# Sample state updates of an SSD decoder step: x and B regrouped by sequence through DRAM, two updates on two 32-row strips of the array

## The chip, the cores and the metric

One core of one Trainium2 chip runs the whole program. The metric is the device time of one execution in microseconds, the median of three runs. The program uses TensorE (PE, with its weight loads shown as PEld), VectorE (DVE), ScalarE (ACT), GpSimd (POOL) and SyncE (SP), which issues most of the DMAs; ACT and POOL issue some too.

## What is computed

The reference is one inference step of a one-layer hybrid decoder, for a prompt of 256 tokens and for 64 sample tokens (8 sequences of 8 tokens, each with a recurrent state of its own). The part around the change is the SSD mixer: a recurrence with 32 heads of 64 channels in 4 groups of 8 heads, with a state of 128 per channel.

```python
# h_t = exp(dt_t a) h_{t-1} + dt_t x_t B_t^T,  y_t = h_t C_t
xdt = (x * dt[..., None])
decay_states = jnp.exp(da_cs[:, :, -1:] - da_cs)
states = jnp.einsum("bcsgn,bcsgr,bcsgrp->bcgrpn", bc, decay_states, xdt)
...
y_off = jnp.einsum("bctgn,bcgrpn,bctgr->bctgrp", cc, states_in, jnp.exp(da_cs))
```

For each of the 8 sample sequences and each of the 4 groups of heads, the new state (128 x 512) is the old one times a decay, plus the product of B (8 tokens x 128) and of x dt decay (8 tokens x 512). Around it stand the projections W_in, W_out, W_up and W_down, all in float32, which are most of the work.

## The kernel before

**The stream of weights.** Every projection is computed transposed: blocks of 128x128 of a weight are the stationary operand, and all 320 tokens (256 + 64) are the moving one. A weight arrives in slabs of 512 KB (`slab`, L110): SP loads one into `wraw`, ACT rounds it to float32r (`whi`, L118), and DVE takes the remainder (`wlo`, L120); each of the three has three buffers. `accumulate` (L127) then makes three matmuls of 128x320 (L129 to L131) for each block, 24 for a slab. I call these the stream; a slab and its load are numbered in the order of the loads (slab 134, load 140).

**The order.** A tile framework puts every engine's instructions into one fixed order when the program is built, by priorities and by its own estimate of times; semaphores enforce what depends on what. DMAs from SP and ACT share eight semaphores, so that a DMA also waits for the one that used its semaphore last. Background work stands in generators that `tick` (L141) advances by one step between slabs. The SSD work of group g is such a generator, `ssd(g)` (L733); it runs between the slabs of W_in and W_out.

**One group of heads** (L733 to L949). SP loads the states of the samples in pairs (`load_state`, L739): `sts[i]` holds sequences i and 4+i, in six buffers `st`; the fourth pair is loaded once the first is stored. x is turned to tokens by PE transposes into PSUM (L762 to L766). For the prompt (c = 0, 1) it is multiplied by dt into `xdt`. For the samples (c = 2, 3: sequences 0 to 3 and 4 to 7), `fourfold` (L359) lets ACT first copy the 32 tokens four times side by side, so that one transpose gives the tokens on four strips of 32 rows; `xq` is x dt decay (L772), and `xsp` holds its float32r part on two strips and the remainder on the other two. B has the same layout in `bsp`, made once for all groups (L714 to L725). Both are split so that a product of the two sums high and low parts over the rows.

Then comes, for each pair i of sequences, `begin(i)` and `end(i)` (L852 to L860):

- `with_c` (L812): four matmuls into `yo_ps`, the old state times C, each on one strip of 32 columns of the array.
- `picked` (L820): ACT multiplies `bsp` by a column of `bsel` that is 1 on the rows of sequence i of each half and 0 elsewhere, into `bm`. That is the mask: all 128 rows take part, and only those of one sequence count.
- `shrunk` (L825): POOL multiplies the two states by their decay.
- `grown` (L831): for each of the two halves h, one matmul of 128x512 `bm[:, h]` by `xsp[:, h]` into a PSUM bank (`up_ps`, L834), which DVE adds to the state (L836).
- `store_state` (L839): ACT issues the two stores.

Between these stand `s_ps` (L806, the state of the prompt's first chunk, which waits for `x0d`, made by POOL in L794), and later the prompt's own products (`y_ps`, L912, pairs of matmuls on the two halves of the array's columns) and `fin_ps` (L938). Small tiles of PSUM come from a pool of four banks (`misc`, L57).

The step sizes dt are made earlier (`steps`, L411) with five blocks of 128 tokens: two of the prompt, one of the samples, and two more that repeat the samples fourfold.

Of the kernel before, what the change touches and what calls it, by code (L numbers as in the profile page):

```python
# [17 lines left out]
P = 128  # L18
# [16 lines left out]
def hybrid_step(  # L35
# [38 lines left out]
    bsel = cp.tile([P, 4], F32, name="bsel")  # L74
# [4 lines left out]
    def masks():  # L79
        make_upper_triangular(nc, upper, 1.0, diag=True)  # L80
        make_lower_triangular(nc, later, 1.0, diag=False)
        make_block_diagonal(nc, bd2, TS)

        for r in range(4):
            rs = slice(32 * r, 32 * r + 32)
            pool.tensor_copy(bsel[rs], bd2[rs, rs].rearrange("p (b t) -> p b t", b=4)[:, :, 0])
        for r in range(2):
            rs = slice(64 * r, 64 * r + 64)
            dve.tensor_tensor(out=upper_s[rs], in0=upper[rs, rs], in1=bd2[rs, rs], op=ALU.mult)
        pool.memset(cmask, 1.0)  # L90
        cm4 = cmask.rearrange("p (h b) i -> p h b i", h=2)
        pool.affine_select(out=cm4, in_=cm4, pattern=[[0, 2], [-8, 4], [1, 32]],
                           compare_op=ALU.is_ge, fill=0.0, base=0, channel_multiplier=0)
        pool.affine_select(out=cm4, in_=cm4, pattern=[[0, 2], [8, 4], [-1, 32]],
                           compare_op=ALU.is_ge, fill=0.0, base=7, channel_multiplier=0)
# [259 lines left out]
    def by_token(ps, x, c):  # L355

        pe.transpose(ps, x[:, P * c:P * c + P], ident)

    def fourfold(out, x, i):  # L359

        act.copy(out.rearrange("p k (q t) -> p k q t", q=4), x[:, :, NP + 32 * i:NP + 32 * i + 32].unsqueeze(2).to_broadcast([P, 4, 4, 32]))
        return out

    with ExitStack() as mctx:
# [40 lines left out]
        dt = op.tile([P, 5, NH], F32, name="dt")  # L405
        nda = op.tile([P, 3, NH], F32, name="nda")
        dec = op.tile([P, 5, NH], F32, name="dec")
# [3 lines left out]
        def steps():  # L411
# [23 lines left out]
            for i in range(2):  # L435
                pool.tensor_copy(dtf[:NH, (3 + i) * P:(4 + i) * P].rearrange("p (q t) -> p q t", q=4),
                                 dtf[:NH, NP + 32 * i:NP + 32 * i + 32].unsqueeze(1).to_broadcast([32, 4, 32]))
            yield
            ps = misc("dt_ps")
            for c in range(5):  # L440
                pe.transpose(ps[:, NH * c:NH * c + NH], dtf[:NH, P * c:P * c + P], ident[:NH, :NH])
            H5 = 5 * NH
            dve.tensor_tensor(out=dt, in0=ps[:, :H5].rearrange("p (c h) -> p c h", c=5),
                              in1=bias_bc.unsqueeze(1).to_broadcast([P, 5, NH]), op=ALU.add)

            e = op.tile([P, 5, NH], F32, name="sp_e")
            q = dec
            z2 = tp.tile([P, NT], F32, tag="pv", name="sp_z2", bufs=4)[:, :5 * NH].rearrange("p (c h) -> p c h", c=5)
            act.activation(e, dt, AF.Abs)
# [11 lines left out]
            dve.scalar_tensor_tensor(out=dt, in0=dt, scalar=0.0, in1=q, op0=ALU.max, op1=ALU.add)  # L461
# [3 lines left out]
            dve.scalar_tensor_tensor(out=da, in0=dt, scalar=-1.0, in1=ea.unsqueeze(1).to_broadcast([P, 5, NH]),  # L465
# [37 lines left out]
            later_s = tp.tile([P, NT], F32, tag="pv", name="later_s", bufs=4)[:NS, :2 * P].rearrange("p (r q t) -> p r q t", r=2, q=4)  # L503
            for r in range(2):
                rs = slice(32 * r, 32 * r + 32)
                pool.tensor_tensor(out=later_s[:, r], in0=later[:NS, rs].unsqueeze(1).to_broadcast([NS, 4, 32]),
                                   in1=bd[:, rs].unsqueeze(1).to_broadcast([NS, 4, 32]), op=ALU.mult)
                pe.matmul(ps[:, (3 + r) * NH:(4 + r) * NH], later_s[:, r].rearrange("p q t -> p (q t)"), da[:NS, 2],
                          start=True, stop=True)
            act.activation(dec.rearrange("p c h -> p (c h)"), ps[:, :H5], AF.Exp)  # L510
            dve.tensor_tensor(out=dt[:, 3:5], in0=dt[:, 3:5], in1=dec[:, 3:5], op=ALU.mult)
# [194 lines left out]
        with tc.tile_pool(name="sd", bufs=1) as sd:  # L706
# [7 lines left out]
            for c in range(4):  # L714
                ps = misc("bt_ps")
                b4 = bT if c < 2 else fourfold(sd.tile([P, 4, P], F32, tag="xde", name="b4", bufs=2), bT, c - 2)
                for g in range(4):
                    by_token(ps[:, P * g:P * g + P], b4[:, g], c if c < 2 else 0)
                if c < 2:
                    act.copy(btok[:, c, :], ps)  # L720
                else:
                    b = bsp[:, c - 2]
                    act.copy(b, ps)
                    for rs in (slice(32, 64), slice(96, P)):
                        dve.tensor_tensor(out=b[rs], in0=ps[rs], in1=b[rs].bitcast(F32), op=ALU.subtract)  # L725
# [7 lines left out]
            def ssd(g):  # L733
# [5 lines left out]
                def load_state(i):  # L739

                    st = [sd.tile([P, 512], F32, tag="st", name="st", bufs=6) for _ in range(2)]
                    for h in range(2):
                        sp.dma_start(st[h], state_ssm[4 * h + i, g])
                    return st

# [10 lines left out]
                def times(out, ps, c, at=slice(0, P), h=slice(0, 8)):  # L756
                    n = h.stop - h.start
                    dve.tensor_tensor(out=by_head(out), in0=by_head(ps),
                                      in1=dt[at, c, h0 + h.start:h0 + h.stop].unsqueeze(2).to_broadcast([at.stop - at.start, n, 64]), op=ALU.mult)

                xsp = sd.tile([P, 2, 512], F32R, tag="xsp", name="xsp", bufs=1)
                for c in range(4):  # L762
                    ps = misc("xt_ps")
                    x4 = xs if c < 2 else fourfold(sd.tile([P, 4, P], F32, tag="xde", name="x4", bufs=2), xs, c - 2)
                    for j in range(4):
                        by_token(ps[:, P * j:P * j + P], x4[:, j], c if c < 2 else 0)  # L766
                    if c < 2:
                        times(xdt[:, c, :], ps, c)
                        continue
                    i = c - 2  # L770
                    xq = sd.tile([P, 512], F32, tag="xde", name="xq", bufs=2)
                    times(xq, ps, c + 1)  # L772
                    act.copy(xsp[:, i], xq)
                    dve.tensor_tensor(out=xsp[64:, i], in0=xq[64:], in1=xsp[64:, i].bitcast(F32), op=ALU.subtract)
                    for r in range(2):
                        at = slice(64 - 64 * r + 32 * i, 96 - 64 * r + 32 * i)
                        times(xdt[at, 2, 256 * r:256 * r + 256], ps[at, 256 * r:256 * r + 256], 2, at, slice(4 * r, 4 * r + 4))
# [25 lines left out]
                yield  # L803

# [7 lines left out]
                def with_c(i, st):  # L812

                    for r in range(2):
                        for h in range(2):
                            row = 64 * r + 32 * h
                            pe.matmul(ps_yo[row:row + 32, :256], cms[:, 4 * h + i, :], st[h][:, 256 * r:256 * r + 256],  # L817
                                      start=i == 0, stop=i == 3, tile_position=(0, row))

                def picked(i):  # L820
                    bm = sd.tile([P, 2, P], F32R, tag="bm", name="bm", bufs=2)
                    act.activation(bm, bsp[:, :, bs].bitcast(F32), AF.Copy, scale=bsel[:, i:i + 1])
                    return bm

                def shrunk(i, st):  # L825
                    with first():
                        for h in range(2):
                            pool.tensor_tensor(out=by_head(st[h]), in0=by_head(st[h]),
                                               in1=tote[:, h0:h0 + 8, 4 * h + i:4 * h + i + 1].to_broadcast([P, 8, 64]), op=ALU.mult)

                def grown(st, bm):  # L831
                    for h in range(2):
                        ps = misc("up_ps")
                        made = pe.matmul(ps, bm[:, h], xsp[:, h], start=True, stop=True)  # L834
                        with first():
                            dve.tensor_tensor(out=st[h], in0=st[h], in1=ps, op=ALU.add)  # L836
                    return made.ins

                def store_state(i, st, by=act):  # L839
                    for h in range(2):  # L840
                        by.dma_start(o_ssm_s[4 * h + i, g], st[h])
# [8 lines left out]
                bms = {}  # L850

                def begin(i):  # L852
                    with_c(i, sts[i])
                    bms[i] = picked(i)
                    shrunk(i, sts[i])

                def end(i, by=act):
                    made = grown(sts[i], bms.pop(i))
# [423 lines left out]
```

## Time and profile before

| | |
|---|---|
| median of three runs | 1796.03 us (1794.56 to 1798.4) |
| the profiled execution, its own time | 1796.18 us |
| its span | 1794.3 us |
| its granted TensorE clock, mean | 0.996 |
| HBM read and written | 275.71 MB and 14.82 MB |
| stage with the SSD work | about 430 to 845 us from the span's start |

The profile page counts busy time by engine, follows the chain of work that ended last, and groups instructions by line. A row of the timeline gives the start, the time from the first start to the last end, the engine, the line, the operation, the tiles (written <- read), the shape and the count; a wait stands in brackets with what ended it. A matmul's duration holds its way through the array as well, so what it takes from the PE is the time from its start to the next one's start.

### The profile page before, as it was taken

How to read it: one execution, taken by the hardware profiler on the slowest of the kernel's cores; microseconds unless marked ns; L12 is line 12 of the kernel's file. 1: busy time of each engine (PE TensorE's matmuls, PEld its weight loads, DVE VectorE, ACT ScalarE, POOL GpSimd, SP SyncE). 2: the span in 40 equal slices, each digit the busy share in tenths (PEclk: the TensorE clock that was granted, in tenths of full speed). 3: DMA queues.
4: the chain of work that ended last, by engine and by line, in shares of the span. 5: the costliest groups of instructions: out<-in, count | busy, mean ns of one | idle time of the engine just before them, and what ended most of it. 6: DMA issues, size and time to landing. Idle time of an engine off the chain costs nothing.

```text
span 1794.3 us, 31172 instructions
## 1 busy us (share of the span) xinstructions
PE 1774.6 (99%) x12200; PEld 1741.1 (97%) x12200; DVE 1185.2 (66%) x2048; ACT 797.8 (44%) x1107; POOL 293.2 (16%) x619
## 2 busy tenths in 40 slices
PE   9999999999999999999999999999999999999998
PEld 8999999999889898999999999999999999999997
DVE  5459664556987969677875474746566575656575
ACT  6444454334545446445555433343434343433335
POOL 3102200000431303104321010111101020101004
PEclk9999999999999999999999999999999999999999
DMA  8646544445665565554554545554554555454542
GB/s 279 193 142 192 161 145 153 154 153 180 198 196 187 166 222 163 172 170 145 167 156 154 151 147 155 154 151 148 155 153 146 152 155 152 149 150 154 153 150 101
DMA packets 222226, 292.56 MB, mean 163 GB/s; under 512 B 16672, under 2 KB 150656, under 8 KB 221888
## 3 DMA queue, kind: packets, MB, share of 16 engines
q1 hardware_dynamic: 209392, 268.12, 49.1%
q10 hardware_dynamic: 10304, 14.82, 2.3%
q0 software_dynamic: 2384, 7.64, 1.4%
q8 instruction: 96, 1.57, 0.4%
q14 instruction: 50, 0.41, 0.1%
HBM read 275.71 MB, written 14.82 MB: 162 GB/s over the span
## 4 chain that ended last, share of the span: by engine, by line
PE 91%; DVE 4%; DMA 3%; issue 1%; ACT 1%; POOL 0%; DVEq 0%; ACTq 0%; POOLq 0%
PE ps L129 20%; PE ps L131 19%; PE ps L130 19%; PE pd L129 9%; PE pd L131 9%; PE pd L130 9%; DMA wraw<-in_w_in 1%; DVE wlo L120 1%; DMA cs<-dacs_d 1%; PE y_ps L912 1%; PE yo_ps L817 0%; PE sg L670 0%; DVE cv L388 0%; PE up_ps L834 0%; DVE cs L897 0%
## 5 line engine op out<-in xcount | busy, mean ns | idle before, releaser
L120 DVE TENSOR_TENSOR wlo<-wraw,whi 128x1024 fp32r<-128x1024 f32 (+1 forms) x474 | 585.4, 1235 | 434.0 <-ACT whi L118 431.9
L118 ACT CAST whi<-wraw 128x1024 fp32r<-128x1024 f32 (+1 forms) x475 | 494.8, 1042 | 715.9 <-PE ps L130 431.5
L129 PE MATMUL ps<-h_hi,whi 128*128 128x320 f32 x2524 | 783.4, 311 | 4.8 <-ACT h_hi L346 2.1
L131 PE MATMUL ps<-h_hi,wlo 128*128 128x320 f32 x2524 | 781.3, 310 | 2.0 <-DVE wlo L120 1.9
L130 PE MATMUL ps<-h_lo,whi 128*128 128x320 f32 x2524 | 780.8, 309 | 0.0
L129 PEld LDWEIGHTS ps<-h_hi,whi 128*128 128x128 f32 x2524 | 475.1, 188 | 8.8 <-issue 2.9
L131 PEld LDWEIGHTS ps<-h_hi,wlo 128*128 128x128 f32 x2524 | 474.9, 188 | 3.8 <-DVE wlo L120 3.1
L130 PEld LDWEIGHTS ps<-h_lo,whi 128*128 128x128 f32 x2524 | 475.2, 188 | 0.7 <-DVE h_lo L546 0.2
L129 PE MATMUL pd<-fhi,whi 128*128 128x320 f32 x704 | 217.5, 309 | 0.0
L130 PE MATMUL pd<-flo,whi 128*128 128x320 f32 x704 | 217.5, 309 | 0.0
L131 PE MATMUL pd<-fhi,wlo 128*128 128x320 f32 x704 | 217.5, 309 | 0.0
L129 PE MATMUL pd<-ohi,whi 128*128 128x320 f32 x448 | 139.8, 312 | 0.0
L131 PE MATMUL pd<-ohi,wlo 128*128 128x320 f32 x448 | 138.8, 310 | 0.0
L130 PE MATMUL pd<-olo,whi 128*128 128x320 f32 x448 | 138.6, 309 | 0.0
L129 PEld LDWEIGHTS pd<-fhi,whi 128*128 128x128 f32 x704 | 132.4, 188 | 0.0
L130 PEld LDWEIGHTS pd<-flo,whi 128*128 128x128 f32 x704 | 132.4, 188 | 0.0
L131 PEld LDWEIGHTS pd<-fhi,wlo 128*128 128x128 f32 x704 | 132.4, 188 | 0.0
L1093 POOL COPY ptf<-pad 128x2 f32<-128x2 f32 x88 | 21.0, 239 | 622.3 <-DVE pad L1081 621.6
L217 DVE TENSOR_TENSOR acc_ffn<-acc_ffn,pd 128x320 f32<-128x320 f32 x160 | 77.5, 484 | 38.3 <-PE pd L131 36.9
L129 PEld LDWEIGHTS pd<-ohi,whi 128*128 128x128 f32 x448 | 84.1, 188 | 1.4 <-issue 0.6
L131 PEld LDWEIGHTS pd<-ohi,wlo 128*128 128x128 f32 x448 | 84.1, 188 | 0.5 <-issue 0.4
L130 PEld LDWEIGHTS pd<-olo,whi 128*128 128x128 f32 x448 | 84.1, 188 | 0.2
(301 smaller groups left out, 1590.3 us busy)
## 6 DMA issues: line engine op xcount, KB each, us to landing
wraw<-in_ffn_w_up SPq DMA_DIRECT2D x176, 512.0 KB, 3.7
wraw<-in_w_in SPq DMA_DIRECT2D x144, 512.0 KB, 3.7
wraw<-in_ffn_w_down SPq DMA_DIRECT2D x88, 512.0 KB, 3.5
wraw<-in_w_out SPq DMA_DIRECT2D x64, 512.0 KB, 3.5
st<-in_state_ssm SPq DMA_DIRECT2D x32, 256.0 KB, 4.1
out_ssm_state_sample<-st ACTq DMA_DIRECT2D x30, 256.0 KB, 3.5
cs<-dacs_d SPq DMA_DIRECT2D x16, 320.0 KB, 4.2
xr<-in_xT SPq DMA_DIRECT2D x4, 640.0 KB, 3.9
```

The source lines that it names most:

```text
L118: act.copy(hi[:, o], raw[:, o])
L120: dve.tensor_tensor(out=lo[:, :m], in0=raw[:, :m], in1=hi[:, :m].bitcast(F32), op=ALU.subtract)
L129: pe.matmul(ps, whi, xhi, start=first, stop=False)
L130: pe.matmul(ps, whi, xlo, start=False, stop=False)
L131: return pe.matmul(ps, wlo, xhi, start=False, stop=last).ins
L217: dve.tensor_tensor(out=acc[:, nb, :], in0=acc[:, nb, :], in1=ps[:, :NT], op=ALU.add)
L912: pe.matmul(ps[64 * i:64 * i + 64, cols], w(hl), x(hl, m, cpx), tile_position=(0, 64 * i), **flags)
L1093: pool.tensor_copy(ptf[:, k, :], pad[:, 256:258])
```

## The change

x and B of the samples get a new layout, and the masks go. Rows of `bsp` and `xsp` are now ordered by token, and within a token by high and low part: sequence s of a half stands on the strip of rows 32 s to 32 s + 31 (8 tokens x 4 combinations of high and low parts). [...] A state update then uses a strip of 32 rows of the array. Of the pairs, half 0 takes sequence i and half 1 takes sequence 4 + (i + 2) % 4 (`strip`), so the two updates of a step stand on two different strips, and both matmuls are issued before the two additions.

`fourfold`, `bsel` and `bm` are gone, and x is turned for the samples by four matmuls with the identity on two halves of the columns (`xs_ps`) in place of eight transposes. dt and the decays have three and four blocks in place of five.

```diff
-    def fourfold(out, x, i):
-        act.copy(out.rearrange("p k (q t) -> p k q t", q=4), x[:, :, NP + 32 * i:NP + 32 * i + 32].unsqueeze(2).to_broadcast([P, 4, 4, 32]))
+    def to_strips(out, src):
+        sp.dma_start(out.bitcast(F32), src.rearrange("(h t) a b n -> (t a b) h n", h=2))
...
-            for c in range(4):
+            for c in range(3):
                 ps = misc("bt_ps")
-                b4 = bT if c < 2 else fourfold(sd.tile([P, 4, P], F32, tag="xde", name="b4", bufs=2), bT, c - 2)
+                n = P if c < 2 else NS
                 for g in range(4):
-                    by_token(ps[:, P * g:P * g + P], b4[:, g], c if c < 2 else 0)
+                    pe.transpose(ps[:n, P * g:P * g + P], bT[:, g, P * c:P * c + n], ident)
...
+            b2 = [sd.tile([P, 512], F32R, tag="xde", name="b2", bufs=2) for _ in range(2)]
+            split(b2[0][:NS], b2[1][:NS], ps[:NS])
+            b_d = dr.tile([NS, 2, 2, 512], F32, name="b_d")
+            for i in range(2):
+                for j in range(2):
+                    act.dma_start(b_d[:, j, i], b2[i][:NS].bitcast(F32))
...
+                def strip(h, i):
+                    return (i + 2 * h) % 4
...
+                ps = misc("xs_ps")
+                for j in range(2):
                     for r in range(2):
+                        at = slice(64 - 64 * r, P - 64 * r)
+                        pe.matmul(ps[at, P * j:P * j + P], xs[:, 2 * r + j, NP:NT], ident, start=True, stop=True,
+                                  tile_position=(0, at.start))
+                xq = sd.tile([P, 512], F32, tag="xde", name="xq", bufs=2)
+                x2 = sd.tile([P, 2, 256], F32R, tag="xde", name="x2", bufs=2)
+                for r in range(2):
+                    at, h = slice(64 - 64 * r, P - 64 * r), slice(4 * r, 4 * r + 4)
+                    times(xq[at, :256], ps[at, :256], 3, at, h)
+                split(x2[:, 0], x2[:, 1], xq[:, :256])
+                x_d = dr.tile([NS, 2, 2, 512], F32, tag="x_d", name="x_d", bufs=2)
+                for r in range(2):
+                    at, h = slice(64 - 64 * r, P - 64 * r), slice(4 * r, 4 * r + 4)
+                    for j in range(2):
+                        act.dma_start(x_d[:, :, j, 256 * r:256 * r + 256], x2[at].bitcast(F32))
+                    times(xdt[at, 2, 256 * r:256 * r + 256], ps[at, :256], 2, at, h)
...
                 yield
+                if g == 0:
+                    to_strips(bsp, b_d)
+                to_strips(xsp, x_d)
                 ps = misc("s1_ps")
...
-                def picked(i):
-                    bm = sd.tile([P, 2, P], F32R, tag="bm", name="bm", bufs=2)
-                    act.activation(bm, bsp[:, :, bs].bitcast(F32), AF.Copy, scale=bsel[:, i:i + 1])
-                    return bm
...
-                def grown(st, bm):
+                def grown(i, st):
+                    ups = [misc("up_ps") for _ in range(2)]
                     for h in range(2):
-                        ps = misc("up_ps")
-                        made = pe.matmul(ps, bm[:, h], xsp[:, h], start=True, stop=True)
+                        at = slice(32 * strip(h, i), 32 * strip(h, i) + 32)
+                        made = pe.matmul(ups[h], bsp[at, h, bs], xsp[at, h], start=True, stop=True, tile_position=(at.start, 0))
+                    for h in range(2):
                         with first():
-                            dve.tensor_tensor(out=st[h], in0=st[h], in1=ps, op=ALU.add)
+                            dve.tensor_tensor(out=st[h], in0=st[h], in1=ups[h], op=ALU.add)
```

84 lines of the change are left out of this document (28 added, 56 removed).

## The prediction, made before the changed kernel ran

> **What bounds the kernel now.** I read the page first: the span, the busy times, and the shares of the chain that ended last.
>
> ```profile
> span 1794.3 us, 31172 instructions
> PE 1774.6 (99%) x12200; PEld 1741.1 (97%) x12200; DVE 1185.2 (66%) x2048; ACT 797.8 (44%) x1107; POOL 293.2 (16%) x619
> PE 91%; DVE 4%; DMA 3%; issue 1%; ACT 1%; POOL 0%; DVEq 0%; ACTq 0%; POOLq 0%
> ```
>
> PE is bound nearly throughout. A busy PE need not be at its peak, so I looked at its pace, in stretches of pure stream (us, then busy time and count of PE, PEld, DVE, ACT and POOL):
>
> ```profile
> 300.00:430.00 130.00, 130.00 (x900) 130.00 (x900) 72.94 (x117) 46.70 (x59) 2.74 (x5) 1.00 0.50 151
> ...
> 1200.00:1600.00 400.00, 400.00 (x2729) 400.00 (x2729) 243.63 (x398) 154.74 (x186) 46.89 (x144) 1.00 0.50 152
> ```
>
> 400 us / 2729 = 0.147 us for a stream matmul, 3.52 us for a slab of 24. Then the waits, of ACT and of PE (total, times, longest):
>
> ```profile
> ACT whi L118 <- PE ps L130: 431.5, 208, 3.6
> ...
> PE s_ps L806 <- POOL xde L794: 1.5, 3, 0.7
> ```
>
> ACT waits for PE before it rounds a weight slab, not PE for ACT: the weights run ahead, and PE hardly waits. So work taken from ACT and DVE is worth nothing while PE covers it, and only two things move the time: what PE itself spends, and new waits of PE, whose order is fixed. In the SSD stage I look for both.
>
> **1. The state updates on strips.** What a pair of updates costs PE today is read from starts:
>
> ```profile
> 457.28 0.31 PE L131 MATMUL ps<-h_hi,wlo 128*128 128x320 f32 x1
> 457.52 0.64 PE L817 MATMUL yo_ps<-st,cb_cms 128*32 128x256 f32 x8
> 458.09 0.73 PE L834 MATMUL up_ps<-xsp,bm 128*128 128x512 f32 x2
> 458.66 0.31 PE L129 MATMUL ps<-h_hi,whi 128*128 128x320 f32 x1
> ...
> 629.78 0.62 PE L834 MATMUL up_ps<-xsp,bm 128*128 128x512 f32 x2
> 630.25 0.31 PE L129 MATMUL ps<-h_hi,whi 128*128 128x320 f32 x1
> ```
>
> Inside the stream a pair takes 630.25 - 629.78 = 0.47 us (0.235 each); behind `yo_ps` 458.66 - 458.09 = 0.57. In the order of the old program 10 of the 16 pairs follow `yo_ps` directly: 10 x 0.57 + 6 x 0.47 = 8.5 us. If two strips run side by side, the second 0.235 goes; 16 x 0.235 = 3.8 us is the most that this part can give. That matmuls on separate strips overlap is seen for strips of columns: the eight `yo_ps` of 256 columns take 0.57 us in all. For strips of rows no row shows it.
>
> But a strip is another shape of the array, and the trace shows a price for changing it: the stream matmul at 457.28 would end its turn at 457.43, and `yo_ps` starts at 457.52, 0.09 later. For the way back I take the matmuls on half the columns:
>
> ```profile
> 688.46 0.31 PE L131 MATMUL pd<-ohi,wlo 128*128 128x320 f32 x1
> 688.70 0.54 PE L912 MATMUL y_ps<-cs,xdt 128*64 128x128 f32 x5
> ...
> 689.40 0.28 PE L912 MATMUL y_ps<-cs,xdt 128*64 128x64 f32 x2
> 689.61 0.41 PE L129 MATMUL pd<-ohi,whi 128*128 128x320 f32 x1
> 689.86 0.31 PE L130 MATMUL pd<-olo,whi 128*128 128x320 f32 x1
> ```
>
> The stream would go on at 688.46 + 0.147 = 688.61, so into the shape costs 688.70 - 688.61 = 0.09; out of it 0.10 for a weight load that nothing hides (689.61 to 689.86 is 0.25, not 0.147) and about 0.1 ahead of it. A pair alone in the stream becomes 0.09 + 0.235 + 0.2 = 0.52 against 0.47, and loses 0.05. A pair behind `yo_ps` already pays one exposed load; it becomes 0.235 + 0.2 = 0.44 to 0.53 against 0.57, and I take a gain of 0.1. Together 10 x 0.1 - 6 x 0.05 = **0.7 us gained**. Bounds: 3.8 gained if the shape change is free; 0.7 - 3.8 = 3.1 lost if the strips run one after the other.
>
> The Trainium skill, TensorEngine Tiling (Array Packing), Key Properties, says that changing the tiling mode drains TensorE, while separate tiles run in parallel. The trace agrees on the drain with the 0.09 above. The skill's TensorE: Matmul & The Clock Gate, Part 3, gives 3.07 times for four strips of 32 rows, 512 wide; no run so far shows strips of rows here.
>
> **2. Fewer transposes.** Eight `xt_ps` of each group go, and four `xs_ps` of 128 columns on half arrays come; and in `steps` two `dt_ps` and one of two `dec_ps` go.
>
> ```profile
> 513.83 1.04 PE L357 MATMUL xt_ps<-ident,xs 128*128 128x128 f32 x8
> ...
> L357 PE MATMUL xt_ps<-ident,xs x32: 271/273/327, 440.7 to 700.0; 128*128 128x128 f32 x32
> ...
> L441 PE MATMUL dt_ps<-ident,dtf x5: 222/222/247, 220.3 to 220.6; 32*128 32x32 f32 x5
> ...
> L508 PE MATMUL dec_ps<-sp_e,later_s x4: 272/273/293, 242.2 to 242.6; 64*128 64x32 f32 x4
> ```
>
> The last of eight transposes ends 0.27 behind its start, so one takes (1.04 - 0.27) / 7 = 0.11 us, eight 0.88. The `y_ps` block above holds 448 columns in 689.61 - 688.61 = 1.00 us; 0.25 of it is the change of shape, which leaves 0.75 / 448 us a column, and two pairs of 128 are 0.43 + 0.25 = 0.68. Gain 0.2 a group, 0.8 in all. B: eight transposes go, four with half the weights come: 0.5. dt: two at 0.06 and half of the 0.4 that four `dec_ps` records take: 0.3. **1.6 us gained**; 0 if the half arrays don't overlap, 2.6 if the shape change is free.
>
> **3. The wait of `s_ps`.** It waits for `x0d` of POOL today, 1.5 us over three groups. The new order has 26 stream matmuls before it in place of 7 + 17 around a transpose, so nothing is nearer. Group 1 (DVE, ACT and POOL, then PE):
>
> ```profile
> 515.84 1.28 DVE L758 TENSOR_TENSOR xdt<-xt_ps,dt 128x512 f32<-128x512 f32 x2
> ...
> 517.76 0.85 DVE L758 TENSOR_TENSOR xdt<-xt_ps,dt 32x256 f32<-32x256 f32 x2
> 518.64 0.69 DVE L774 TENSOR_TENSOR xsp<-xq,xsp 64x512 fp32r<-64x512 f32 x1
> ...
> 519.47 1.04 POOL L794 TENSOR_TENSOR xde<-xdt,dec 128x512 f32<-128x512 f32 x1 [8.86 <-DVE xsp L774]
> ...
> 518.08 0.61 PE L780 MATMUL cb_ps<-cT,bT 128*128 128x128 f32 x4
> 518.62 0.34 PE L783 MATMUL cb_ps<-cT,bT 128*64 128x64 f32 x4
> 520.57 1.12 PE L806 MATMUL s_ps<-xde,btok 128*128 128x512 f32 x2 [0.39 <-POOL xde L794]
> ```
>
> `x0d` takes the buffer of `xq`, so it waits for the split. New: `xdt` until 517.1, two `xq` and two `xdt` at 0.42 until 518.8, the remainder of 256 columns (half of 0.69, estimated 0.4) until 519.2, `x0d` until 520.3. PE gets there at 513.83 + 0.88 + 0.68 + 0.8 (`cb_ps`, from 518.08 to the end of its last rows) + 26 x 0.147 = 520.0. It still waits 0.3: **0.3 us gained** in all, 0 to 1.5.
>
> **4. The way through DRAM: the new wait.** The first `up_ps` of a group needs `xsp` back from DRAM, and PE holds everything behind it. Continue group 1. ACT issues the first store behind the remainder, at 519.2. Between it and the other three the new order puts the rounding of weight slab 137, which waits for PE to end slab 134 (two matmuls ahead of the 520.0 above: 519.7).
>
> ```profile
> 525.91 1.05 ACT L118 CAST whi<-wraw 128x1024 fp32r<-128x1024 f32 x1 [3.59 <-PE ps L130]
> ...
> 528.82 0.94 ACTq L841 DMA_DIRECT2D out_ssm_state_sample<-st  x2
> ...
> out_ssm_state_sample<-st ACTq DMA_DIRECT2D x4, 256.0 KB, 3.7
> out_y<-acc_ffn ACTq DMA_DIRECT2D x1, 160.0 KB, 2.0
> wraw<-in_w_in SPq DMA_DIRECT2D x4, 512.0 KB, 4.3
> cs<-dacs_d SPq DMA_DIRECT2D x3, 320.0 KB, 5.9
> ```
>
> The rounding takes 1.05 (until 520.75), three issues 0.47 each (until 522.15). A store of 128 KB lands after 2.0 (160 KB on a quiet queue) to 3.7 (256 KB here); I take 2.5: 524.65. SP waits there, with weight load 141 behind it, which isn't due before slab 138 is split, around 527.5: nothing lost. The load of 512 KB takes 4.3 like a weight slab here, to 5.9: 529.0, at the latest about 531.8. PE: `s_ps` 520.3 + 1.05, `yo_ps` 0.57, 22 matmuls, `yo_ps` 0.57, 24 matmuls = 529.3. **A dead heat.** The three other groups have the same chain and nearly the same distance (69 to 90 stream matmuls). A chain of this length that arrives on time on average is late half of the time; I take 0.5 us a group, **2.0 us lost**; 0 to 2.5 a group, so 0 to 10.
>
> **5. Two waits from the new order.** In groups 1 to 3 the first update moved behind one more slab and stands right by the second. (a) With `yo_ps` held, two of four small banks remain after the first pair, and its additions (0.68 each) must free one: about 0.25 a group, **0.8 us lost**, 0 to 3. (b) In groups 2 and 3 the fourth state pair loads into the buffers of the first, and the last `yo_ps` follows soon:
>
> ```profile
> 711.00 0.73 PE L834 MATMUL up_ps<-xsp,bm 128*128 128x512 f32 x2
> 711.82 1.27 DVE L836 TENSOR_TENSOR st<-st,up_ps 128x512 f32<-128x512 f32 x2
> 712.53 0.94 ACTq L841 DMA_DIRECT2D out_ssm_state_sample<-st  x2
> 715.01 0.89 SPq L743 DMA_DIRECT2D st<-in_state_ssm  x2
> ...
> st<-in_state_ssm SPq DMA_DIRECT2D x32, 256.0 KB, 4.1
> ```
>
> From update to loaded: 715.01 + 4.1 - 711.00 = 8.1 us, and half 1 loads behind a weight slab, say 9.1. The new order leaves 48 stream matmuls and four small blocks, 7.0 + 2.0 = 9.0. I take 0.3 twice, **0.6 us lost**, 0 to 3.
>
> **Costed at nothing.** ACT loses 16 maskings, 10 fourfold copies and the casts of `xsp`, and gets 20 issues at 0.47; DVE loses some 12 us. PE covers both, as the waits show; gone, a cover would cost at most an issue's length in front of a late slab, 0.47. The x traffic of 0.5 MB a group each way is little where DMA is half idle. POOL's copies of `bsel`, `dtf` and `later_s` stand in stages where PE runs.
>
> **Sum**, against the profiled execution of 1796.18 us (span 1794.3 and 1.9 around it), which lies 0.15 over the median: -0.7 - 1.6 - 0.3 + 2.0 + 0.8 + 0.6 = +0.8; 1797.0, as a median **1796.8 us**. A measurement of this kernel tells about 0.2%, 3.6 us, from no change.
>
> **Rivals.** (A) Strips gain in full: changes of shape hidden behind weight loads, `xsp` in time. -3.8 - 2.6 - 0.3 + 0.8 + 0.6 = -5.3: 1790.7. For it: the column strips overlap; against it: each change of shape in the trace shows its gap. (B) **Slower: x comes late.** If a group's stores and its load land at the slow ends, each first update waits 2.5, not 0.5: +0.8 + 8 = +8.8, 1804.8. It decides from the point where `xsp` lands later than about 13.5 us behind the last `xs_ps`. For it: six steps on four queues, of which each can slip; against it: every duration I took is a median of this stage. (C) The change doesn't do what it says: row strips run in turn, +0.8 + 3.8 = +4.6: 1800.6. No row speaks against it.
>
> **Chances.** Forecast 0.49, A 0.16, B 0.25, C 0.10. Faster by over 0.2%: A, 0.16. Slower by over 0.2%: B and C, 0.35. Within: 0.49. The range reaches to A and B: 1790.7 to 1804.8. The forecast's own range is 1793 to 1799.5.
>
> **What would show it.** Step 1: the two `up_ps` start within hundredths of each other, and the stream follows 0.4 to 0.5 behind; 0.235 between them would be C. Step 2: `xs_ps` takes 0.7. Step 4: PE's list of waits names `up_ps` and the DMA into `xsp`, with under 1 us each; above 2 is B. Step 5: short waits of `up_ps` for DVE's additions and of `yo_ps` for the state load. The forecast is wrong if anything outside 430 to 845 us moves.

## The result, and the profile after

| | before | changed |
|---|---|---|
| median of 20 runs each, side by side | 1794.17 us (1790.32 to 1798.85) | 1799.21 us (1795.82 to 1803.44) |
| ratio | | 1.0029, 95% interval 1.0022 to 1.0036 |
| profiled execution, its own time; span | 1796.18; 1794.3 us | 1798.01; 1796.3 us |
| stage: slab 105 to slab 212 of PE | 455.4 us | 460.5 us |
| the rest: slab 212 to slab 471 | 912.99 us | 912.95 us |
| HBM read and written | 275.71 and 14.82 MB | 278.33 and 17.45 MB |

The changed kernel is 0.29% slower, 5.0 us; I had forecast 0.8. The time lies in the range (1790.7 to 1804.8; it was reckoned from 1796.03, and from this comparison's 1794.17 it would be 1788.8 to 1802.9), but the class that I gave the most weight, no measurable change, is not what came. A stage is counted from the start of the first matmul of one weight slab of the stream to that of another (405.0 to 860.3 us before, 401.9 to 862.4 after). It is some 5 us longer. Ahead of it the two profiled executions differ by 2.8 us the other way, within the first ten slabs; the changed kernel, profiled once more, differs from itself there by 2.0 (e7). A second pair of traces (e7 and e4) has the stage 8.2 us longer, 2.0 less ahead of it and 1.1 less behind it. So the loss lies in the stage, but a pair of traces tells its size to some 3 us only; the 5.0 rests on the medians.

The page and PE's list of waits of the changed kernel (waits: total, times, longest, in us; its line numbers are its own, not those of the kernel before):

```profile
span 1796.3 us, 31118 instructions
PE 1776.8 (99%) x12192; PEld 1737.1 (97%) x12192; DVE 1171.4 (65%) x2033; ACT 779.3 (43%) x1074; POOL 291.3 (16%) x612
PE 90%; issue 5%; DMA 2%; DVE 1%; ACT 0%; POOL 0%; ACTq 0%; SPq 0%; DVEq 0%; POOLq 0%
```

```profile
PE s_ps L809 <- POOL xde L794: 4.0, 2, 3.5
...
PE ps L124 <- DVE pad L376: 1.1, 1, 1.1
...
PE yo_ps L820 <- DMA st<-in_state_ssm: 0.7, 1, 0.7
```

By the page's count DVE has 14 us less to do and ACT 19 less: the relief came, and it bought nothing: PE is busy 2 us longer and idle as long as before (19.5 and 19.7 us of the span). In the stage, though, PE's waits rise from 3.2 to 4.7 us, not counting those at its end that both kernels have. The wait of `s_ps`, which I had costed as 0.3 us better, holds 3.5 us in one place, group 0. The timeline of the changed kernel there:

```profile
436.04 0.66 PE L764 MATMUL xs_ps<-ident,xs 128*64 128x128 f32 x8
...
436.68 2.44 ACTq L714 DMA_DIRECT2D b_d<-b  x4
...
443.35 0.86 DVE L750 TENSOR_TENSOR xq<-xs_ps,dt 64x256 f32<-64x256 f32 x2 [4.80 <-DMA b_d<-b]
...
444.54 0.40 ACT L338 CAST x<-xq 128x256 fp32r<-128x256 f32 x1 [3.15 <-DMA b_d<-b]
...
446.49 1.04 POOL L794 TENSOR_TENSOR xde<-xdt,dec 128x512 f32<-128x512 f32 x1 [59.31 <-DMA cs<-dacs_d]
...
446.91 2.22 ACTq L776 DMA_DIRECT2D x_d<-x  x3
447.58 1.12 PE L809 MATMUL s_ps<-xde,btok 128*128 128x512 f32 x2 [3.46 <-POOL xde L794]
...
453.48 0.36 SPq L356 DMA_DIRECT2D xsp<-x_d  x1
```

In the changed kernel x goes through DRAM: `x2`, the split x dt decay, leaves by four stores of ACT into `x_d` and comes back as `xsp` by one load of SP; B goes once, by `b2` and `b_d` into `bsp`. The last rows of x are out of `xs_ps` at 436.7, but DVE writes `xq` only at 443.35: it waits for the stores of B. `b2`, `xq`, `x2` and `x0d` (xde) share two buffers by their tag, and B's two parts lie in both until their stores have landed. (POOL's bracket names a DMA of `cs`; that is only the last semaphore it sat behind. The row above it shows who was late: `x2`, read from `xq`, before `x0d` may take `xq`'s buffer.) Then the clock. The granted TensorE clock is the third number from the right in these two stretches behind that wait:

```profile
450.00:452.00 2.00, 2.00 (x9) 2.00 (x9) 0.00 (x0) 1.46 (x2) 2.00 (x3) 0.51 0.97 345
452.00:454.00 2.00, 2.00 (x15) 2.00 (x15) 1.34 (x5) 0.00 (x0) 1.62 (x2) 1.00 1.00 344
```

From 448.5 to 452 us the clock is about half, and a stream matmul takes 0.267 us in place of 0.147; seven of those, and 0.6 us in the block itself, make some 1.5 us on top of the wait. The Trainium skill, TensorE: Matmul & The Clock Gate, Part 1: The HAM clock gate, says that the clock halves after an idle window of about 3.4 us and comes back after a busy one; the trace agrees, with 0.51 behind 3.46 us. But e1 shows the same behind 2.85 us and e7 does not, so the length of the stop alone does not decide (see the last section).

To see every place, I took PE's blocks between stretches of stream: from the start of the last stream matmul to the start of the next, less 0.147, and what the next one still takes over 0.147. Sums of these, us:

| | before | changed | changed, second trace (e7) |
|---|---|---|---|
| group 0: `s_ps` with the first `yo_ps` | 2.61 | 5.97 | 4.74 |
| group 0: the other updates and `yo_ps` | 4.16 | 4.42 | 5.26 |
| groups 1 and 2: `s_ps` with the first `yo_ps` | 2.27 and 2.27 | 1.94 and 1.93 | 1.94 and 1.94 |
| group 1: updates, `yo_ps` | 4.15 | 4.55 | 4.57 |
| group 2: updates, `yo_ps` | 4.17 | 5.85 | 5.87 |
| group 3: `s_ps` with the first `yo_ps` | 1.85 | 2.47 | 2.45 |
| group 3: updates, `yo_ps` | 3.69 | 5.55 | 7.02 |
| blocks with x's and B's transposes | 17.1 | 16.0 | 16.0 |
| all blocks of the stage | 75.1 | 80.5 | 81.7 |

Group 0 holds 3.6 of the 5.4 us by which the blocks differ in the first pair, and the updates of groups 2 and 3 hold 3.5; the transposes and the `s_ps` of groups 1 and 2 give 1.8 back, and the blocks of `y_ps` 1.0, most of it a wait that the second trace of the kernel before lacks (e4).

Group 2's 1.7 us are mostly the wait that I had foreseen for the fourth state pair, at 0.3 (a row of the changed kernel; PE's bracket gives the part without the weight load):

```profile
628.09 0.49 PE L833 MATMUL up_ps<-xsp,bsp 32*128 32x512 f32 x2
...
633.54 0.63 PE L820 MATMUL yo_ps<-st,cb_cms 128*32 128x256 f32 x6 [0.70 <-DMA st<-in_state_ssm]
```

And the two strips do run side by side. The pair that stands alone in the stream, in the changed kernel:

```profile
477.57 0.31 PE L126 MATMUL pd<-ohi,wlo 128*128 128x320 f32 x1
477.81 0.49 PE L833 MATMUL up_ps<-xsp,bsp 32*128 32x512 f32 x2
478.23 0.41 PE L124 MATMUL pd<-ohi,whi 128*128 128x320 f32 x1
478.48 0.31 PE L125 MATMUL pd<-olo,whi 128*128 128x320 f32 x1
```

The two `up_ps` start 0.003 to 0.004 us apart in 13 of the 16 pairs (0.22 to 0.34 in the kernel before), and both end within 0.49 us of the first one's start (two full ones took 0.62). But the pair takes 478.23 - 477.57 - 0.147 = 0.51 us from the stream, and the next stream matmul 0.10 more: 0.61 to 0.62, against 0.46 before.

### The profile page after: what moved, and what is told of

Same layout as the page of the kernel before. It is cut to its first block, busy times and chain, and to the rows that moved or that the text cites. A ratio compares the mean times of both kernels' runs of the same rounds, so it can differ in the third digit from the quotient of the medians.

```text
span 1796.3 us, 31118 instructions
## 1 busy us (share of the span) xinstructions
PE 1776.8 (99%) x12192; PEld 1737.1 (97%) x12192; DVE 1171.4 (65%) x2033; ACT 779.3 (43%) x1074; POOL 291.3 (16%) x612
## 3 DMA queue, kind: packets, MB, share of 16 engines
q8 instruction: 96, 1.57, 0.3%
HBM read 278.33 MB, written 17.45 MB: 165 GB/s over the span
## 4 chain that ended last, share of the span: by engine, by line
PE 90%; issue 5%; DMA 2%; DVE 1%; ACT 0%; POOL 0%; ACTq 0%; SPq 0%; DVEq 0%; POOLq 0%
PE ps L124 18%; PE ps L126 18%; PE ps L125 18%; PE pd L124 10%; PE pd L125 10%; PE pd L126 10%; PE y_ps L909 1%; PE yo_ps L820 1%; PE sg L658 0%; DMA wraw<-in_w_in 0%; PE up_ps L833 0%; DMA lg<-in_gate_ln_g 0%; PE tsum L258 0%; DVE wlo L115 0%; DMA st<-in_state_ssm 0%
## 5 line engine op out<-in xcount | busy, mean ns | idle before, releaser
L115 DVE TENSOR_TENSOR wlo<-wraw,whi 128x1024 fp32r<-128x1024 f32 (+1 forms) x474 | 585.5, 1235 | 441.3 <-ACT whi L113 439.4
```

Of the source, the lines that this page charges most:

```text
L115: dve.tensor_tensor(out=lo[:, :m], in0=raw[:, :m], in1=hi[:, :m].bitcast(F32), op=ALU.subtract)
```

## The experiments

My theory after the first trace: the loss is the shared buffers in group 0. Rivals: the traffic there, the length of x's own chain, and the strips' changes of shape. All ratios are to the kernel before on the same chip.

### e7 and e4: both kernels again

The changed kernel, unedited. 

> The changed kernel once more, as the measure for e5 and e6 on one chip and for a second trace: 1.0029 on the kernel before; s_ps waits 3.3 to 3.7 us in group 0, and the two waits that the first trace of it lacked (convolution padding behind 507, y_ps for cs behind 593) are there or not as chance has it.

Measured: 1.0033 (1.0023 to 1.0044), stage 460.8 us. PE's waits:

```profile
PE s_ps L809 <- POOL xde L794: 3.4, 2, 2.8
...
PE yo_ps L820 <- DMA st<-in_state_ssm: 2.2, 2, 1.5
...
PE up_ps L833 <- DMA xsp<-x_d: 0.8, 1, 0.8
```

The loss repeats, but it moves: 0.7 us less at `s_ps`, 0.8 at `up_ps` for x from DRAM, 1.5 more for states. Two of the three are waits for a DMA, and the third, as shown above, stands behind one.

The kernel before, unedited, run once. 

> The kernel before once more, for a second trace of it. Two of its waits are gone in the changed kernel: the stream's wait for the padding of the convolution (1.2 us, near 507 us from the span's start) and y_ps's wait for cs (1.1 us, near 593). If the relief of DVE and ACT takes them away, both stand in this trace too, within 0.3 us; if they are the chance of one execution, at least one of them is missing or differs by more than 0.5.

Measured: 1796.39 us, stage 452.6 us against 455.4 in the first trace. The two waits, from the first trace of the kernel before (the expectation calls the first one the convolution's padding, the row names `acc_mix`; its sizes, 1.2 and 1.1, count the weight load behind the wait too):

```profile
PE ps L129 <- DVE acc_mix L217: 0.9, 1, 0.9
PE y_ps L912 <- DVE cs L901: 0.8, 1, 0.8
```

Neither stands in the second. They were the chance of one execution, so the relief of DVE takes no credit for them. The first trace of before is 2.8 us longer in this stage: these two waits, 2.3 us, and a low clock near the stage's end for 6.8 us in place of 3.4, against which e4 has some 0.7 us more in its waits for weight slabs.

### e1: B in a buffer of its own

```diff
-            b2 = [sd.tile([P, 512], F32R, tag="xde", name="b2", bufs=2) for _ in range(2)]
-            split(b2[0][:NS], b2[1][:NS], ps[:NS])
+            b2 = sd.tile([P, 512], F32R, name="b2")
+            split(b2[:NS], b2[NS:], ps[:NS])
```

> The changed kernel with one edit: b2, the high and low part of B, gets a buffer of its own in place of the two xde buffers; PE's order stays as it is but for one matmul. Theory (shared buffers): group 0's xq, x2 and x0d stand behind the four stores of B only because they take b2's buffers, so the 3.46 us wait of s_ps for x0d falls below 0.5, the slow pace of PE right behind it goes too, the block from s_ps to yo_ps falls from 5.7 us to some 2.5, and of the 5.0 us that the change lost against the kernel before (1.0029) some 3.4 come back: +1.6 us, 1.0009. Rival (traffic): x0d is late because four stores, the state loads and the cs loads fill the queues and engines at that place; then the wait stays above 2 us and the time at +4 to +5, 1.0025 or more.

Measured: 1.0020 (1.0009 to 1.0031): by the medians 1.6 us of the 5.0 are back, half of what the theory said. The interval holds the rival's 1.0025 too, so the trace has to decide. PE's wait of `s_ps` in group 0 is gone (0.33 us), and another has come in its place, from the timeline of e1:

```profile
440.77 1.05 ACT L113 CAST whi<-wraw 128x1024 fp32r<-128x1024 f32 x1 [3.68 <-PE ps L125]
441.73 0.40 ACT L338 CAST x<-xq 128x256 fp32r<-128x256 f32 x1
...
447.00 0.52 ACTq L776 DMA_DIRECT2D x_d<-x  x1
...
453.03 0.36 SPq L356 DMA_DIRECT2D xsp<-x_d  x1
...
457.09 0.50 PE L833 MATMUL up_ps<-xsp,bsp 32*128 32x512 f32 x2 [2.85 <-issue]
```

x's last store is issued by 447.5, `xsp`'s load at 453.0, 4.0 us later it is there, and PE has stood for 2.85 us; the clock falls to 0.51 here too (458.8 to 462.2). Behind the last `xs_ps` `xsp` is there after 20.1 us, in the changed kernel after 20.7: the edit hardly moved it. So the shared buffers were the first of two waits in a row: in the changed kernel the stop at `s_ps` hid the late `xsp`. My theory was true of the wait and false of the time.

### e9: B's way left out

```diff
-                    act.dma_start(b_d[:, j, i], b2[i][:NS].bitcast(F32))
+            pool.tensor_copy(bsp, btok)
...
-                if g == 0:
-                    to_strips(bsp, b_d)
```

> The changed kernel without B's half of the way: four stores into b_d and the load of bsp (0.5 MB each way, once, in group 0) are left out and bsp is filled with other data (left out: B's regrouped values); the rest and PE's order stay, and b2 still takes the xde buffers. Theory (in group 0 the wait is traffic: B's 1 MB beside states, weights and cs): s_ps's 3.5 us go, and xsp comes back in time too, so that no wait of up_ps takes its place as it did in e1; 3.4 us or more under the changed kernel, 1.0010 on the kernel before. Rival (x's own chain is too long for its place): up_ps waits 2 us or more for xsp, as in e1: 1.0020.

Measured: 1.0000 (0.9990 to 1.0009): 5.2 us under the changed kernel, and nothing waits in group 0. The timeline of e9:

```profile
440.32 0.41 ACT L338 CAST x<-xq 128x256 fp32r<-128x256 f32 x1 [2.33 <-DVE xq L747]
441.10 0.41 DVE L339 TENSOR_TENSOR x<-xq,x 128x256 fp32r<-128x256 f32 x1
...
441.80 2.74 ACTq L773 DMA_DIRECT2D x_d<-x  x4
...
445.14 1.02 PE L804 MATMUL s_ps<-xde,btok 128*128 128x512 f32 x2
```

x's last store is issued by 444.5, against 447.5 in e1 and 449.1 in the changed kernel; counted from the start of slab 105, which differs between the runs, 41.3, 45.2 and 47.2 us. It does not land faster: the medians of x's stores in 436 to 460 us are, for the changed kernel and for e9,

```profile
x_d<-x ACTq DMA_DIRECT2D x4, 128.0 KB, 5.1
```

```profile
x_d<-x ACTq DMA_DIRECT2D x4, 128.0 KB, 6.1
```

With 1 MB less the stores took longer, if anything. So the theory as I had put it, that B costs by its traffic, finds no support here; B costs by where its stores stand. Its four issues (2.44 us of ACT in the changed kernel) and its hold on the buffers push x's split back: in e1, where the buffers are its own, x's cast stands at 441.7, behind the rounding of a weight slab that waits for PE, and in e9 ahead of it. B's stores also hold x's issues, by the eight shared semaphores. In e1 three of x's four stores are issued within 0.1 us behind the landing of the DMA that had used their semaphore last: the first (443.96) behind B's second store (443.88), the third (445.37) behind B's fourth (445.35), the last (447.00) behind a load of `cs` (446.98). How much each of the two costs, no run separates.

### e8 and e10: without the way, strips or full rows

e8 also leaves out x's stores and loads, and fills `xsp` once. PE's order falls back to that of the kernel before. e10 is e8 with full rows:

```diff
-                        at = slice(32 * strip(h, i), 32 * strip(h, i) + 32)
-                        made = pe.matmul(ups[h], bsp[at, h, bs], xsp[at, h], start=True, stop=True, tile_position=(at.start, 0))
+                        made = pe.matmul(ups[h], bsp[:, h, bs], xsp[:, h], start=True, stop=True)
```

> The changed kernel without the way through DRAM: the stores into b_d and x_d and the loads of bsp and xsp are left out, and bsp and xsp are filled once with other data (left out: the regrouped values, so the sample states are not the reference's). x2 is still made. Without the load PE's fixed order sets the first update of groups 1 to 3 where the kernel before had it. Theory (nearly all of the loss is the way: its waits, its traffic, and the order that it forces): the strips that are left cost 0.6 us (10 pairs behind yo_ps gain 0.035 each, 6 alone lose 0.16 each), fewer transposes gain 1.8, the waits of s_ps some 0.6: 0.9990 on the kernel before. Rival (strips and changes of shape are the loss): at least +2 us, 1.0011 or above.

> As e8, with each update as a matmul over all 128 rows (left out: as in e8, and the choice of the sequence). The pair to e8, without DRAM waits to blur it. Theory (a strip's changes of shape eat its overlap): full rows are 0.6 us faster than e8, since six pairs that stand alone fall from 0.62 to 0.46 and ten behind yo_ps rise by 0.035; equal within what the runs can tell. Rival A of the prediction (overlap in full): 3.8 us slower than e8, 0.0021 more.

Measured: e8 0.9989 (0.9979 to 0.9998), stage 451.4 us; e10 0.9984 (0.9975 to 0.9993), stage 450.0 us. A pair alone in e8, then in e10:

```profile
473.81 0.31 PE L126 MATMUL pd<-ohi,wlo 128*128 128x320 f32 x1
474.05 0.50 PE L823 MATMUL up_ps<-xsp,bsp 32*128 32x512 f32 x2
474.47 0.41 PE L124 MATMUL pd<-ohi,whi 128*128 128x320 f32 x1
474.73 0.31 PE L125 MATMUL pd<-olo,whi 128*128 128x320 f32 x1
```

```profile
472.62 0.31 PE L126 MATMUL pd<-ohi,wlo 128*128 128x320 f32 x1
472.77 0.62 PE L822 MATMUL up_ps<-xsp,bsp 128*128 128x512 f32 x2
473.23 0.31 PE L124 MATMUL pd<-ohi,whi 128*128 128x320 f32 x1
```

Into the strip 0.09 (474.05 - 473.81 - 0.147), then 0.42 to the stream's return where one strip's columns alone take 0.235, then 0.11: a pair costs 0.62, and full rows 473.23 - 472.62 - 0.147 = 0.46. Behind `yo_ps` it is 1.20 with strips and 1.24 with full rows. The intervals of e8 and e10 overlap, but the blocks with `up_ps`, without the mixed last one, say what rival A denied: 15.1 us with strips and 14.6 with full rows, so strips are 0.5 us dearer here, not 3.8 cheaper. (All blocks, 72.9 and 71.7 us, differ by 1.2, but 0.4 of that is a wait of `y_ps`, and 0.4 lies in the last block, where other work stands between.) The way through DRAM is the whole loss and more: 1.0029 less 0.9989, 7.2 us, of which B's part is 5.2 (e9) and x's 2.0, by medians; the blocks of e9 and e8 (75.0 and 72.9 us) agree with the 2.0. In e9 x's part shows in PE's order: groups 1 to 3 take 15.0 us for updates and `yo_ps` in e9, 12.2 in e8.

### e2 and e3: one strip, and full rows in the changed kernel

e2 has `return i` in `strip`; e3 has the edit of e10 in the changed kernel.

> The changed kernel with one edit: half 1 takes the same strip as half 0 (sequence 4 + i in place of 4 + (i + 2) % 4), so both updates of a step stand on one strip; PE's order is the same. Theory (two strips run side by side): the second up_ps now starts 0.23 behind the first in place of 0.01, 16 x 0.22 = 3.5 us more than the change: +8.5 us on the kernel before, 1.0047. Rival C of the prediction (strips run in turn): nothing to lose, +5.0, 1.0029.

> The changed kernel with one edit: each update is a matmul over all 128 rows of bsp and xsp, without strip or mask, in PE's same order (left out: the choice of the sequence, so each state gets the sum of four sequences' updates). Theory (a change of shape costs more than I took, and eats what the strips save): eight updates that stand alone in the stream fall from 0.62 to 0.47 us, 1.2 us less; those right by yo_ps cost 0.05 more each, 0.4 more: about 0.8 us less than the change, +4.2 on the kernel before, 1.0023. Rival A of the prediction (strips gain in full, 0.235 for each pair): full rows cost 3.8 more, +8.8, 1.0049.

Measured: e2 1.0047 (1.0035 to 1.0060), as the theory had it. That shuts out rival C's 1.0029, but not e7's whole interval on the same chip (1.0023 to 1.0044), and e2's trace stands 4.2 us at `s_ps` in group 0, more than either trace of the changed kernel. So the pairs have to show it; one alone in e2:

```profile
482.58 0.31 PE L126 MATMUL pd<-ohi,wlo 128*128 128x320 f32 x1
482.82 0.73 PE L833 MATMUL up_ps<-xsp,bsp 32*128 32x512 f32 x2
483.48 0.42 PE L124 MATMUL pd<-ohi,whi 128*128 128x320 f32 x1
```

0.66 from its start to the stream's, where two strips take 0.42, and the two starts are 0.34 us apart, not 0.003: the overlap is real, 0.24 a pair. e3 measured 1.0035 (1.0022 to 1.0047), between theory and rival, and tells nothing by its time: its `s_ps` in group 0 happened to wait 4.1 us. Its blocks are those of e10 (0.46 alone, 1.24 behind `yo_ps`).

### e5 and e6: x earlier

e5 gives `xq` a buffer and puts the block from `xs_ps` to x's stores, unchanged, ahead of the loop with `xt_ps`; e6 moves the split to POOL as well, and stores x once:

```diff
-                split(x2[:, 0], x2[:, 1], xq[:, :256])
+                pool.tensor_copy(x2[:, 0], xq[:, :256])
+                pool.tensor_tensor(out=x2[:, 1], in0=xq[:, :256], in1=x2[:, 0].bitcast(F32), op=ALU.subtract)
```

> The kernel with B's own buffer (e1), and three edits beside it: xq lies in a buffer of its own, the four xs_ps matmuls and the split of x come ahead of the eight xt_ps, and by that PE's fixed order sets the first update of groups 1 to 3 six matmuls ahead of the second, not right by it. In e1 group 0 waited 2.85 us at up_ps for xsp's load, which SP issued at 453.0, 5.5 us behind the last store's issue at 447.5. Theory (the way through DRAM starts too late in ACT's and DVE's order): the last store is issued some 1.4 us sooner, so the wait falls to about 1.4; the waits for a bank in groups 1 and 2 (0.35 each) and for the fourth state pair in group 2 (1.2) lose 0.7 and 0.9 more, and the waits of s_ps go (0.9): about 3.5 us under e1 (1.0020), 1.0000 on the kernel before. Rival (the traffic sets when xsp lands, whatever the order): the wait stays at 2.5 or more, and the time at 1.0012 or above.

> As e5, with two edits more: POOL does both parts of x's split, so that they don't stand behind the rounding of weight slabs; and x goes to DRAM once (two stores of 128 KB in place of four, x_d half as large), while two loads of 256 KB write its rows twice. Theory (order and traffic at the end of group 0's chain): the last store is issued some 4 us ahead of e1's; the wait at up_ps falls under 1.3, where what is left is SP's weight load that stands ahead of the second load until 451: 0.9995 on the kernel before. Rival (DMA traffic alone): 0.25 MB less at some 280 GB/s is worth 0.9 us, so the wait stays near 2 and the time within 0.0005 of e5 plus or minus.

Measured: e5 1.0067 (1.0048 to 1.0085), e6 1.0027 (1.0014 to 1.0041). Both forecasts failed, e5 by 12 us. Its ACT and SP, in group 0:

```profile
446.73 3.19 ACTq L770 DMA_DIRECT2D x_d<-x  x3
...
449.96 1.05 ACT L113 CAST whi<-wraw 128x1024 fp32r<-128x1024 f32 x1 [3.96 <-DMA x_d<-x]
...
450.28 0.55 ACTq L770 DMA_DIRECT2D x_d<-x  x1
...
456.15 0.37 SPq L110 DMA_DIRECT2D wraw<-in_w_out  x1
...
456.69 0.38 SPq L356 DMA_DIRECT2D xsp<-x_d  x1
```

B's four issues still stood ahead (441.3 to 443.7). Three issues for x then hold ACT from 446.7 to 449.9, and the fourth comes at 450.3. Here too three of the four come within 0.1 us behind the landing of the DMA that had used their semaphore last: B's first store (446.65) and two state loads (449.39 and 450.21).

The two traces can be compared only from a common start: slab 105 begins at 406.45 in e5 and at 402.36 in e1. Counted from there, x's last store is issued 0.8 us sooner than in e1 and lands 1.4 us sooner, near what I had forecast. It didn't help, since SP issues a weight load first: `xsp`'s load leaves 1.1 us behind that landing (0.1 in e1) and takes 4.7 us (4.0 in e1), and PE is there 0.5 us sooner. So group 0's first update waits 3.7 us, not 1.4; group 3's, now six matmuls sooner, waits 2.3, and group 2's last `yo_ps` 2.8 for its states. Around the end of the first of these stops the clock is half for 6.8 us, behind group 2's for 3.4. e6 waits 2.8 us for `xsp` in group 0, with 6.8 us of half clock there, and 2.3 in two places for states.

### e11 and e12: B's way early

The first part of the edit stands at the end of `steps`, near 250 us, with B's split and stores behind it; the second is the first line of the SSD stage. e12 also stores x once and loads it with two DMAs.

```diff
+            yield
+            ps = misc("bt_ps")
+            for g in range(4):
+                pe.transpose(ps[:NS, P * g:P * g + P], bT[:, g, NP:NT], ident)
...
+            to_strips(bsp, b_d)
```

> The changed kernel with B's way moved out of the crowd: the sample part of B (final at 168 us in the trace) is turned, split and stored to b_d behind the step sizes, near 250 us, and bsp is loaded first of all in the SSD stage, ahead of the states. Nothing is left out. Theory (e9: in group 0 it is B's traffic and its hold on the xde buffers that cost 5 us, not B's work): s_ps waits under 1 us in group 0, up_ps doesn't wait for xsp, and the time is e9's 1.0000 plus at most 0.0008 for the 0.5 MB load that now stands ahead of the states; 1.0004 on the kernel before. Rival (any B load near the states delays them or xsp as much): the yo_ps or up_ps of group 0 waits 2 us or more for a DMA, 1.0020 or above.

> As e11, with x stored once (two stores of 128 KB a group in place of four) and read twice (two loads of 256 KB). Theory (what is left of the way's cost in groups 1 to 3, some 2 us by e9 less e8, is PE's order, which the estimate of xsp's return sets, and not traffic): the same as e11 within 0.0006. Rival (traffic of x's stores): 0.25 MB less a group takes 0.0005 or more off.

Measured: e11 1.0005 (0.9996 to 1.0014), with nothing left out; all but 0.9 us of the loss is back. e12 1.0027 (1.0016 to 1.0037): neither theory nor rival. In e11's group 0, from its timeline and its list of waits:

```profile
440.63 0.55 ACTq L782 DMA_DIRECT2D x_d<-x  x1
441.61 2.72 ACTq L782 DMA_DIRECT2D x_d<-x  x3
...
444.67 1.02 PE L813 MATMUL s_ps<-xde,btok 128*128 128x512 f32 x2
```

```profile
PE up_ps L837 <- issue: 1.2, 1, 1.2
```

x's stores are all issued by 444.3, as in e9, and `s_ps` is on time; `xsp` is 1.2 us late. e12's longest new wait, in group 3, is for a state pair:

```profile
727.23 0.63 PE L824 MATMUL yo_ps<-st,cb_cms 128*32 128x256 f32 x6 [1.58 <-DMA st<-in_state_ssm]
```

Its blocks hold 2.3 us more than e11's (78.9 and 76.6), most of it in that block (2.96 for 1.16). The medians differ by 3.8. In the traces the clock is half for 10.2 us near the end of the stage in e12 and for 6.8 in e11, which may be chance; why the state pair is later, and what makes up the rest, stays open. No version with all its work beats the kernel before, and e10, which leaves work out, shows the most there was to win: 0.16%.

## Why the prediction was right or wrong

- **Bounds and stage: right.** PE bounds the kernel, work taken from DVE and ACT bought nothing, and nothing behind the stage grew (912.99 and 912.95 us; 914.00 in the second trace of before).
- **Step 1, the strips: mechanism right, size wrong, and with it the sign.** The two updates overlap (rival C falls, though its 4.6 us stand next to the measured 5.0; that is chance), and a change of shape eats it (rival A falls). The way out of the shape was the mis-sized term: 0.2 in my sum, 0.42 - 0.235 = 0.19 ahead of the load and 0.10 to 0.11 in it as measured, 0.29. A pair alone loses 0.16, not 0.05; one behind `yo_ps` gains 0.035, not 0.1. For ten and six pairs that is 6 x 0.16 - 10 x 0.035 = 0.6 us lost in place of 0.7 gained; e8 and e10 show 0.5 for five and ten.
- **Step 2, fewer transposes: right in sum, wrong inside.** 1.1 us in the stage and 0.5 ahead of it, 1.6 as forecast. But B's part gave some 0.8 (0.5 forecast), dt 0.5 (0.3), and x's 0.1 or less a group (0.2): a block of half arrays between full ones costs nearly what it saves. The right sum is luck.
- **Step 3, the wait of `s_ps`: this step failed.** I worked it out for group 1, where it held (0.2 us left, 0.3 forecast), and carried it to the others. In group 0 the tiles `b2` (two of them), `xq`, `x2` and `x0d` share two buffers, and the wait rose to 3.46 us, 5 with the slow clock. In group 3, where nothing waited before, it is 0.6. The diff showed both the tag and B's stores.
- **Step 4, the dead heat: the lateness is real, the place wrong.** "The three other groups have the same chain and nearly the same distance": in groups 1 to 3 `xsp` was there 12.9 to 14.0 us behind the last `xs_ps` and 1.2 to 2.2 us ahead of the first update, in both traces, and cost nothing where 0.5 a group was forecast. Group 0 has B's four stores, two state loads and three `cs` loads in front, and needs 20 to 21 us. There the update waited 0.8 us in the second trace, and 2.85 in e1; in the changed kernel step 3's wait hides it. So rival B's lateness came, but in one group only.
- **Step 5, the new order: right, too small.** The bank wait is in group 1's 0.40 and group 2's share (0.25 forecast); the state wait made group 2's last `yo_ps` and update 2.50 for 1.24, and group 3's `yo_ps` 1.37 or 2.84 for 0.77, by execution.
- **Costed at nothing: failed for ACT's issues.** I priced an issue by what it takes in front of a weight slab, 0.47, not by what it pushes x's own chain back. It is the place of B's stores that B's 5 us hang on (e9, e11): with B's way early they are gone, though its 0.5 MB load still stands ahead of the states.

What is not settled: how far the late landings in group 0 (5 to 6 us for 128 KB against 2.4 in the median of all groups) come from the crowd of loads. e9 took 1 MB of B's away and they stayed.

## What to carry to other kernels

When a value goes on a new way, walk the way in each of its instances, the first above all, where one-time work of the same change stands in the same buffers and on the same queue. Two waits in a row hide each other: take away the first and the second gets its turn, so a fix is priced by what is late next, not by the wait in the list. Compare the times of two traces from a common point of the work, here the start of a slab: by their own clocks e5's last store comes 3.3 us later than e1's (450.3 and 447.0), by the stream's 0.8 us sooner. And count a change of the array's shape twice, in and out (here 0.09 and 0.29 us), before giving an overlap its gain.

## What the hardware showed that I had not expected

- The granted clock fell to half behind idle times of 3.46 us (changed kernel) and 2.85 us (e1), and not behind one of 2.85 us in e7. In every trace the low stretches start whole multiples of 3.41 us apart and, but for the one that the program's end cuts off, last 3.41 us or a multiple of it. On that grid 2.4 us of the changed kernel's idle time and 1.7 of e1's lie in the one stretch just ahead of the low one; e7's are split into 1.40 and 1.45 us over two stretches, and 1.57 us in one stretch (e12's stop at 727 us) were not enough. My reading of these four, not tried by itself: about half of one such stretch has to be idle, so it is partly chance whether a stop of this length costs another 1.5 us.
- Near the end of the stage, around PE's stop of 2.1 us there, the clock is low in every trace, for 3.4, 6.8 or 10.2 us, in the kernel before too (6.8 and 3.4). So 1.5 us between two traces of the stage say nothing of the kernel.
- Two updates of 32x128 by 32x512 on two strips take 0.42 us to the stream's return, on one strip 0.66; over all 128 rows two take 0.46 with no exposed load. For two strips between full-array work the overlap pays less than the shape costs.
